# A two-layer decoder step on eight cores: all 2176 tokens resident, one pass over the weights, a column-tiled convolution and norm sums on VectorE

## The chip, the cores and the metric

The kernel runs on all eight cores of one Trainium2 chip: two dies, cores 0 to 3 and 4 to 7. Every core does the same work on its own tokens (one prompt of 2048 tokens and 16 samples of 8 tokens, so 2176), without exchange between cores. The metric is the time in microseconds (us) of the slowest core.

The chip has a second, slower state, in which the cores of one die show a lower granted TensorE clock, whatever the kernel: in e13's rounds the kernel before took 3559.17 us in one run, with clocks of 0.80 to 0.81 on one die and 0.96 on the other, and 3045.06 us in another; e1 took 3120.24 us with 0.84 and 0.98, and 2725.1 us with 0.98 on both.

Engines: PE is TensorE, PEld its weight loads, DVE VectorE, ACT ScalarE, POOL GpSimd, SP SyncE. In a line, the output stands left of the arrow.

## The reference, cut to what matters

```python
def trunk(x, p, ...):                     # 2 layers; D = 1024
    for i in range(2):
        x = x + 0.5 * swiglu(rmsnorm(x, norm_ffn[i, 0]), ...)      # width 2816
        h = rmsnorm(x, norm_mix[i])
        x = x + (even_mixer(h, ...) if i == 0 else odd_mixer(h, ...))
        x = x + 0.5 * swiglu(rmsnorm(x, norm_ffn[i, 1]), ...)
        gate = sigmoid(rmsnorm(x, norm_ple[i]) @ w_ple_gate[i])
        emb = rmsnorm(p[i] @ w_ple_proj[i], norm_ple_proj[i])
        x = x + gate * emb
    return rmsnorm(x, norm_final), ...    # and the new states

def even_mixer(h, ...):
    proj = h @ w_in                       # xa (512), va (512), ga (512)
    pa = <trailing means over 2, 4, 8, 16 tokens of xa, a 128x128 map per group, a scale>
    u = va * sigmoid(ga)
    conv = <causal depthwise convolution of u, 31 taps per channel>
    yb = silu(layernorm(conv + dw_bias))
    return concatenate([pa, yb]) @ w_out
```

Tokens lie along the free axis and channels on the partitions, so a sum over channels (every norm) runs over eight chunks and across partitions. The kernel before does all of it by eight ones-matmuls on TensorE; the changed one adds the chunks on VectorE and leaves one.

## The kernel before

It works in two token groups (1152 and 1024 tokens), each in three blocks, and streams all weights once for each group. The parts that the argument touches:

```python
# norm: eight squares on ScalarE, eight ones-matmuls, square root, reciprocal, eight scalings
def norm_squares(blk):
    for c in range(8):
        act(H[:, c, c0:c0 + n], X[:, c, c0:c0 + n], AF.Square)
def s_stats():
    mm_group(pb[:, 0:n], [(ONES[:, :], H[:, c, c0:c0 + n]) for c in range(8)])
    act(sd[:, 0:n], pb[:, 0:n], AF.Sqrt, bias=NORM_EPS, scale=1.0 / D)
    dve_recip(rs[:, 0:n], sd[:, 0:n])
# ... cut ...
# even mixer, convolution: 31 diagonal 128x128 matrices for each of four channel groups
for bi, (c0, n) in enumerate(blocks):
    for j in range(4):
        pairs = [(DIAG[:, j * 31 + k, :], UXP[:, j, c0 + k:c0 + k + n]) for k in range(31)]
        mm_group(pb[:, 0:n], pairs)
        # ... cut: V, VB (bf16 copy) and VSQ by three ScalarE instructions ...
    # ... cut: pooled projection, sums for the layer norm, layer norm ...
# ... cut ...
for g in range(2):                        # two token groups
    W.reset()                             # every weight is streamed again
    if g == 0:
        for blk in blocks:
            x_block_final(blk, "norm_ffn00")   # squares of all three blocks first
    for l in range(2):
        ffn(l, 0, ...); even_mixer(g, ...) or odd_mixer(g, ...); ffn(l, 1, ...); ple(l, ...)
```

Of the kernel before, what the change touches and what calls it, by code (L numbers as in the profile page):

```python
# [11 lines left out]
D = 1024  # L12
DFF = 2816
NHC = DFF // 128
SEQ = 2048
NS = 16
TS = 8
PLE = 256
GCOLS = [1024 + NS * TS, 1024]
GOFF = [0, GCOLS[0]]  # L20
TCOLS = sum(GCOLS)
MAXC = max(GCOLS)
SLOT = 3072
NSLOT = 6
NORM_EPS = 1e-6
LN_EPS = 1e-5
HPARTS = [list(range(0, 11)), list(range(11, 22))]

PCOL = {}
_pc = 0  # L30

def _padd(name, n):
    global _pc
    PCOL[name] = _pc
    _pc += n

# [12 lines left out]
_padd("dw_w", 4 * 31)  # L49
_padd("sc_w", 8 * 3)  # L50
_padd("ident", 128)
NPAR = _pc

def weight_tile_list():
    tiles = []
    for l in range(2):
        def ffn(f):
            for hp, part in enumerate(HPARTS):
                for m in part:
                    tiles.append((("gu", l, f, m), 8 * 256))  # L60
                for i in range(0, len(part), 3):
                    ch = part[i:i + 3]
                    tiles.append((("dn", l, f, tuple(ch)), len(ch) * 1024))
        ffn(0)
        if l == 0:
            for j in range(4):
                tiles.append((("ine_vg", j), 8 * 256))
            for j in range(2):
                tiles.append((("ine_xa", j), 8 * 256))
            tiles.append((("pp",), 4 * 128))  # L70
            for ch in ((0, 1, 2), (3, 4, 5), (6, 7)):
                tiles.append((("oute", ch), 8 * 128 * len(ch)))
        else:
            for c in range(8):
                tiles.append((("ino", c), 8 * 384))
            for ch in ((0, 1, 2), (3, 4, 5), (6, 7)):
                tiles.append((("outo", ch), 8 * 128 * len(ch)))
        tiles.append((("plep", l), 2 * 1024))
        ffn(1)
        for ch in ((0, 1, 2), (3, 4, 5), (6, 7)):  # L80
            tiles.append((("pleg", l, ch), 8 * 128 * len(ch)))
    return tiles

def _kc(w):
    k, n = w.shape
    return w.reshape(k // 128, 128, n).transpose(1, 0, 2)

def pack_weights(inp):
# [4 lines left out]
    for key, n in tiles:  # L93
# [10 lines left out]
        elif kind == "ine_vg":  # L104
# [3 lines left out]
                                _kc(w[:, 1024 + j * 128:1024 + (j + 1) * 128])], axis=2)  # L108
        elif kind == "ine_xa":
            j = key[1]  # L110
            w = inp["w_in_even"][0]
            t = _kc(w[:, j * 256:(j + 1) * 256])
# [14 lines left out]
        elif kind == "plep":  # L127
            t = _kc(inp["w_ple_proj"][key[1]])
        elif kind == "pleg":
# [8 lines left out]
    return out  # L138

def pack_params(inp):  # L140
# [17 lines left out]
    dw = inp["dw_weight"][0]  # L158
    p[:, PCOL["dw_w"]:PCOL["dw_w"] + 124] = dw.T.reshape(4, 128, 31).transpose(1, 0, 2).reshape(128, 124)
    sc = inp["sc_weight"][0]  # L160
    p[:, PCOL["sc_w"]:PCOL["sc_w"] + 24] = sc.T.reshape(8, 128, 3).transpose(1, 0, 2).reshape(128, 24)
    p[:, PCOL["ident"]:PCOL["ident"] + 128] = np.eye(128, dtype=np.float32)
    return p

def _fm(a):
    t, f = a.shape
    return a.T.reshape(f // 128, 128, t).transpose(1, 0, 2)

def pack_core(inp, i):
    xp = inp["x_prompt"][i]  # L170
    xs = inp["x_sample"][i * NS:(i + 1) * NS]
    xs_tm = xs.transpose(1, 0, 2).reshape(NS * TS, D)
    xT = np.concatenate([_fm(xp[:1024]), _fm(xs_tm), _fm(xp[1024:])], axis=2)
    pts = []
    for l in range(2):
        pp = inp["p_prompt"][l, i]
        ps = inp["p_sample"][l, i * NS:(i + 1) * NS].transpose(1, 0, 2).reshape(NS * TS, PLE)
        pts.append(np.concatenate([_fm(pp[:1024]), _fm(ps), _fm(pp[1024:])], axis=2))
    pT = np.stack(pts, axis=1)

    def st(a):
# [5 lines left out]
        "pT": np.ascontiguousarray(pT.reshape(128, 4, TCOLS), dtype=np.float32),  # L187
# [4 lines left out]

ENGS = ("pe", "act", "dve", "pool", "sp")
EPOCH = 30000

class Sched:
    def __init__(self):
# [7 lines left out]
        self.label = ""  # L205
        self.pe_labels = []
# [3 lines left out]
    def reg(self, handle, arena, base):  # L210
        self.arena[handle.name] = (arena, base, mybir.dt.size(handle.dtype))

    def region(self, ap):
        name = ap.tensor.name
        if name not in self.arena:
            return None
        arena, base, es = self.arena[name]
        pat = list(ap.ap)
        pstride = pat[0][0]
        off = ap.offset % pstride if pstride > 0 else ap.offset  # L220
# [3 lines left out]
        return arena, base + off * es, base + (off + ext) * es  # L224
# [35 lines left out]
    def op(self, eng, fn, reads=(), writes=(), dma_sem=None, extra_deps=(), dma_total=None):  # L260
# [11 lines left out]
        for ap in reads:  # L272
            r = self.region(ap)
            if r is not None:
                self._access(r[0], r[1], r[2], ticket, False, deps)
        for ap in writes:
            r = self.region(ap)
            if r is not None:
# [30 lines left out]

def build_program():  # L310
# [4 lines left out]

    d_xT = nc.dram_tensor("xT", [128, 8, TCOLS], F32, kind="ExternalInput").ap()
    d_pT = nc.dram_tensor("pT", [128, 4, TCOLS], F32, kind="ExternalInput").ap()
# [4 lines left out]
    d_gpr = nc.dram_tensor("gpprow", [128, 2, D], F32, kind="ExternalInput").ap()  # L322
    d_w = nc.dram_tensor("wts", [128, WTOT], F32, kind="ExternalInput").ap()
    d_yT = nc.dram_tensor("yT", [128, 8, TCOLS], F32, kind="ExternalOutput").ap()
# [10 lines left out]
    def alloc(name, shape, dt, arena=None, at=None):  # L335
        nbytes = int(np.prod(shape[1:])) * mybir.dt.size(dt)
        if at is None:
            off = cur[0]
            cur[0] += (nbytes + 63) // 64 * 64
            assert cur[0] <= top, (name, cur[0], top)  # L340
        else:
            off = at
        h = nc.alloc_sbuf_tensor_at(name, list(shape), dt, offset=off)
        S.reg(h, arena or "sb", off)
        return h

    X = alloc("x", [128, 8, MAXC], F32)
    H = alloc("h", [128, 8, MAXC], BF16)
    HID_BYTES = 11 * MAXC * 2
    hid_off = cur[0]  # L350
    HID = alloc("hid", [128, 11, MAXC], BF16)
    UXP = alloc("uxp", [128, 4, 30 + 1024], BF16, at=hid_off)
    o1 = (hid_off + 4 * (30 + 1024) * 2 + 63) // 64 * 64
    UXS = alloc("uxs", [128, 4, 38 * NS], BF16, at=o1)
    o2 = (o1 + 4 * 38 * NS * 2 + 63) // 64 * 64
    V = alloc("v", [128, 4, 512], F32, at=o2)
    assert o2 + 4 * 512 * 4 <= hid_off + HID_BYTES
    YCAT = alloc("ycat", [128, 8, MAXC], BF16, at=hid_off)
    RING = alloc("ring", [128, NSLOT, SLOT], BF16)
    DIAG = alloc("diag", [128, 4 * 31, 128], BF16)  # L360
    PT = alloc("pt", [128, 4, MAXC], BF16)
# [3 lines left out]
    IDB = alloc("idb", [128, 128], BF16)  # L365
    RC = alloc("rc", [128, 16], F32)
    vb_off = cur[0]
    VB = alloc("vb", [128, 4, 512], BF16)
    VSQ = alloc("vsq", [128, 4, 512], BF16)
    ESQ2 = alloc("esq2", [128, 8, 512], BF16, at=vb_off)  # L370
    STP = alloc("stp", [128, 4, 15 * NS], F32)
    STSC = alloc("stsc", [128, 8, 2 * NS], F32)
    PTAIL = alloc("ptail", [128, 4, 16], F32)
    UTAIL = alloc("utail", [128, 4, 32], BF16)
    ZTAIL = alloc("ztail", [128, 8, 2], F32)
    O_PS = alloc("o_ps", [128, 4, TS * NS], F32)
    O_DS = alloc("o_ds", [128, 4, TS * NS], F32)
    O_DP = alloc("o_dp", [128, 4, 32], F32)
    O_SS = alloc("o_ss", [128, 8, 2 * NS], F32)
    NSCR = 10  # L380
    SCW = 528
    SCR = [alloc(f"scr{i}", [128, SCW], F32) for i in range(NSCR)]
    RSE = alloc("rse", [128, MAXC], F32)
    LRS = alloc("lrs", [128, 512], F32)
    LRS2 = alloc("lrs2", [128, 512], F32)
    NRS = [alloc("nrs0", [128, 512], F32)] * 2
    nrs_i = [0]
    scr_i = [0]

    def scratch():  # L390
        t = SCR[scr_i[0] % NSCR]
        scr_i[0] += 1
        return t

    PS = []
    for i in range(8):
        p = nc.alloc_psum_tensor(f"ps{i}", [128, 512], F32)
        S.arena[p.name] = ("ps", i * 2048, 4)
        PS.append(p)
    ps_i = [0]  # L400

    def bank():
        p = PS[ps_i[0] % 8]
        ps_i[0] += 1
        return p
# [4 lines left out]
    def act(out, in_, func, bias=None, scale=None, extra_reads=()):  # L410
        kw = {}
        rd = [in_] + list(extra_reads)
# [8 lines left out]
        S.op("act", lambda e: e.activation(out=out, in_=in_, func=func, **kw), reads=rd, writes=[out])  # L421
# [9 lines left out]
    def dve_ts(out, in0, s1, s2, op0, op1=None):  # L431
        rd = [in0] + [s for s in (s1, s2) if s is not None and not isinstance(s, float)]
        if op1 is None:
            S.op("dve", lambda e: e.tensor_scalar(out=out, in0=in0, scalar1=s1, scalar2=None, op0=op0),
                 reads=rd, writes=[out])
        else:
            S.op("dve", lambda e: e.tensor_scalar(out=out, in0=in0, scalar1=s1, scalar2=s2, op0=op0, op1=op1),
                 reads=rd, writes=[out])

    def pool_tt(out, in0, in1, op):  # L440
        S.op("pool", lambda e: e.tensor_tensor(out=out, in0=in0, in1=in1, op=op), reads=[in0, in1], writes=[out])  # L441
# [3 lines left out]

    def dve_recip(out, in_):
        S.op("dve", lambda e: e.reciprocal(out=out, in_=in_), reads=[in_], writes=[out])  # L447
# [6 lines left out]
    def mm_group(ps_ap, pairs, extra_reads=()):  # L454
        n = len(pairs)
# [646 lines left out]
```

## Time and profile before

| | before |
|---|---|
| time, median of 4 runs | 3042.43 us (3040.2 to 3043.48) |
| profiled span, slowest core | 3043.2 us |
| PE busy | 2786.7 us, 92%, 17664 matmuls |
| PE idle | 256 us |
| VectorE, ScalarE busy | 1254.2 and 802.8 us |
| bytes read from memory by a core | 371 MB |

How to read it: PE is the engine to watch, because it is busy for 92% of the span. The kernel can only become faster by less PE work or by less PE idleness. The prediction below shows the lines.

### The profile page before, as it was taken

The numbers are of one execution on the slowest core, as the hardware profiler recorded it, in microseconds if no ns is written. First come the engines' busy times: TensorE is split into PE (matmuls) and PEld (weight loads), VectorE is DVE, ScalarE is ACT, GpSimd is POOL, SyncE is SP. The second block draws the span as 40 slices with busy tenths as digits, with TensorE's granted clock in tenths as the row PEclk, the third lists the DMA queues.
The fourth block names the chain that finished last, engine by engine and source line by source line (L and its number), as shares of the span: only waits on it lengthen the run. The fifth ranks groups of instructions, "written<-read, shape, count | busy, mean of one in ns | idle before, by whom it ended". The sixth has DMA issues, their size and how long they took to land.

```text
span 3043.2 us, 42462 instructions; the slowest of 8 cores (3031.3 to 3043.2 us)
## 1 busy us (share of the span) xinstructions
PE 2786.7 (92%) x17664; PEld 1499.0 (49%) x17664; DVE 1254.2 (41%) x2381; ACT 802.8 (26%) x1599; POOL 263.7 (9%) x407
## 2 busy tenths in 40 slices
PE   2999998999889999999973999989997999999996
PEld 0555443554445545455431555545554555555553
DVE  2432555232632257523354224552326222862335
ACT  2102344221330122321242112352224202232224
POOL 0000000000220000000031000000002100000003
PEclk7999998999999999999996999999999999999998
DMA  6433411534142534153325542405341534424332
GB/s 142 80 56 59 66 26 28 87 49 77 25 75 47 100 51 76 30 87 56 69 63 128 87 73 49 66 15 94 56 77 25 105 66 73 91 42 87 63 63 73
DMA packets 62495, 204.32 MB, mean 67 GB/s; under 512 B 8288, under 2 KB 15072, under 8 KB 62304
## 3 DMA queue, kind: packets, MB, share of 16 engines
q0 software_dynamic: 44592, 179.16, 34.5%
q1 hardware_dynamic: 17712, 22.45, 2.6%
q8 instruction: 139, 2.28, 0.3%
q14 instruction: 52, 0.43, 0.1%
HBM read 371.06 MB, written 10.62 MB: 125 GB/s over the span
## 4 chain that ended last, share of the span: by engine, by line
PE 82%; DVE 9%; ACT 3%; DMA 3%; issue 1%; SPq 1%; POOL 0%; ACTq 0%; DVEq 0%; POOLq 0%
PE ps L460 82%; DVE h L428 4%; DVE nrs_83 L447 2%; ACT h L421 2%; DMA x<-xT 2%; DVE x L428 1%; SPq L470 1%; DMA ring<-wts 1%; DVE x L424 1%; DVE lrs_82 L447 0%; DVE v L424 0%; ACT L421 0%; DVE ring L424 0%; POOL x L441 0%; ACT v L421 0%
## 5 line engine op out<-in xcount | busy, mean ns | idle before, releaser
L460 PE MATMUL ps<-h,ring 128*128 128x512 bf16 (+2 forms) x11352 | 1797.9, 320 | 56.5 <-DVE h L428 33.8
L460 PEld LDWEIGHTS ps<-h,ring 128*128 128x128 bf16 x11352 | 965.1, 99 | 871.7 <-issue 65.8
L460 PE MATMUL ps<-hid,ring 128*128 128x512 bf16 (+2 forms) x4224 | 656.7, 317 | 0.8 <-DVE hid L424 0.5
L460 PEld LDWEIGHTS ps<-hid,ring 128*128 128x128 bf16 x4224 | 356.1, 98 | 299.8 <-issue 1.1
L470 POOL DMA_DIRECT2D ring<-wts x298 | 157.8, 534 | 2539.3 <-PE ps L460 2504.3
L428 DVE SCALAR_TENSOR_TENSOR x<-ps,x 128x512 f32<-128x512 f32 (+2 forms) x384 | 200.0, 532 | 342.0 <-PE ps L460 339.2
L421 ACT ACTIVATE h<-x 128x512 bf16<-128x512 f32 (+2 forms) x432 | 200.4, 499 | 456.5 <-DVE x L428 269.0
L460 PE MATMUL ps<-h,ones 128*128 128x512 bf16 (+2 forms) x432 | 99.8, 389 | 142.4 <-ACT h L421 141.8
L428 DVE SCALAR_TENSOR_TENSOR h<-x,par,nrs_83 128x512 bf16<-128x512 f32 (+2 forms) x384 | 214.1, 606 | 1.7
L460 PEld LDWEIGHTS ps<-h,ones 128*128 128x128 bf16 x432 | 42.1, 115 | 192.5 <-ACT h L421 153.2
L421 ACT ACT_TABLE_LOAD x87 | 111.6, 1283 | 46.6 <-PE ps L460 44.3
L460 PE MATMUL ps<-pt,ring 128*128 128x512 bf16 (+2 forms) x384 | 80.9, 329 | 45.6 <-DVE ring L424 29.6
L460 PE MATMUL ps<-uxp,diag 128*128 128x512 bf16 (+2 forms) x620 | 108.5, 336 | 0.0
L421 ACT ACTIVATE scr_78<-ps 128x512 f32<-128x512 f32 (+2 forms) x91 | 42.1, 463 | 219.7 <-PE ps L460 211.4
L421 ACT ACTIVATE scr_76<-ps 128x512 f32<-128x512 f32 (+2 forms) x76 | 36.2, 476 | 233.9 <-PE ps L460 228.1
L421 ACT ACTIVATE scr_74<-ps 128x512 f32<-128x512 f32 (+2 forms) x87 | 41.3, 474 | 173.0 <-PE ps L460 164.8
L421 ACT ACTIVATE scr_72<-ps 128x512 f32<-128x512 f32 (+2 forms) x87 | 40.8, 469 | 169.5 <-PE ps L460 166.8
L421 ACT ACTIVATE scr_77<-ps 128x512 f32<-128x512 f32 (+2 forms) x90 | 42.5, 472 | 157.5 <-PE ps L460 148.8
L421 ACT ACTIVATE scr_79<-ps 128x512 f32<-128x512 f32 (+2 forms) x84 | 41.0, 488 | 156.7 <-PE ps L460 155.3
L421 ACT ACTIVATE scr_73<-ps 128x512 f32<-128x512 f32 (+2 forms) x90 | 41.9, 466 | 147.8 <-PE ps L460 139.3
L460 PEld LDWEIGHTS ps<-uxp,diag 128*128 128x128 bf16 x620 | 55.1, 97 | 52.3
L421 ACT ACTIVATE scr_70<-ps 128x512 f32<-128x512 f32 (+2 forms) x91 | 43.1, 474 | 136.6 <-PE ps L460 132.4
(261 smaller groups left out, 1361.1 us busy)
## 6 DMA issues: line engine op xcount, KB each, us to landing
ring<-wts POOLq DMA_DIRECT2D x216, 512.0 KB, 8.1
ring<-wts POOLq DMA_DIRECT2D x80, 768.0 KB, 7.2
x<-xT SPq DMA_DIRECT2D x32, 256.0 KB, 7.0
yT<-x SPq DMA_DIRECT2D x24, 256.0 KB, 2.1
yT<-x SPq DMA_DIRECT2D x8, 192.0 KB, 1.9
pt<-pT POOLq DMA_DIRECT2D x4, 288.0 KB, 22.6
pt<-pT POOLq DMA_DIRECT2D x4, 256.0 KB, 12.3
yT<-x SPq DMA_DIRECT2D x16, 64.0 KB, 1.6
```

Source lines behind the costliest of these rows:

```text
L421: S.op("act", lambda e: e.activation(out=out, in_=in_, func=func, **kw), reads=rd, writes=[out])
L424: S.op("dve", lambda e: e.tensor_tensor(out=out, in0=in0, in1=in1, op=op), reads=[in0, in1], writes=[out])
L428: S.op("dve", lambda e: e.scalar_tensor_tensor(out=out, in0=in0, scalar=scalar, in1=in1, op0=op0, op1=op1), reads=rd, writes=[out])
L447: S.op("dve", lambda e: e.reciprocal(out=out, in_=in_), reads=[in_], writes=[out])
L460: ins = e.matmul(ps_ap, l, r, start=(i == 0), stop=(i == n - 1))
L470: S.op(eng, lambda e: e.dma_start(out=out, in_=in_), reads=[in_], writes=[out], dma_sem=sem, dma_total=total, extra_deps=extra)
```

## The change

Its intent: to take matmuls away (convolution, norm sums, embedding norms), and to let tokens wait for nothing, by keeping all of them in SBUF in five blocks (four of 512 tokens, one of 128) and streaming each weight once. The program is emitted by a small scheduler: pieces of a norm are put on a heap with a model time and placed in the engines' queues when the modelled PE time has come (`defer`), or when the block is needed (`ensure`).

```diff
-        for c in range(8):                                   # norm before
-            act(H[:, c, c0:c0 + n], X[:, c, c0:c0 + n], AF.Square)
-            mm_group(pb[:, 0:n], [(ONES[:, :], H[:, c, c0:c0 + n]) for c in range(8)])
-            act(sd, pb, AF.Sqrt, ...); dve_recip(rs, sd)
+    class Norm:                                              # norm after
+        def chunk(self, mo, lag=0.8): ...                    # square, then:
+            dve_tt(self.acc[:, 0:n], self.acc[:, 0:n], sq[:, 0:n], ALU.add)
+            # ... after the eighth chunk one ones-matmul, then
+            act(rs[:, 0:n], self.pb[:, 0:n], AF.Abs_reciprocal_sqrt, bias=NORM_EPS)
 ...
+        def load_r(j, b):                     # even mixer: the shifted copy
+            for s in range(4):                # partitions 32s.. hold the row shifted by s
+                for q in range(4):            # 32 channels each
+                    items.append(("sp", RALL[32 * s:32 * s + 32, j, q, 0:L], src))
 ...
-                    pairs = [(DIAG[:, j * 31 + k, :], UXP[:, j, c0 + k:c0 + k + n]) for k in range(31)]
+                for m in range(8):            # 4 taps at once on the 4 x 32 input rows
+                    for q in range(4):        # 4 column tiles of 32 channels
+                        ops.append((pb[32 * q:32 * q + 32, 0:n], DG[:, 4 * j + q, m, :],
+                                    RALL[:, j, q, 4 * m * st:4 * m * st + n], m == 0, m == 7))
 ...
+                dve_copy(vv[:, 0, 0:n], V[:, j, 0:n])        # bf16 copy, now on VectorE
+                if b + 1 < NB:
+                    load_r(j, b + 1)
 ...
-    for g in range(2):
-        W.reset()
+    n0 = [Norm(b, "norm_ffn00") for b in range(NB)]
+    for mo in range(8):
+        n0[0].chunk(mo)
+    for b in range(1, NB):
+        for mo in range(8):
+            defer(6.0 + 12.0 * (b - 1) + 0.9 * mo, lambda b=b, mo=mo: n0[b].chunk(mo), ("n", b))
```

(The whole change touches most of the program.) The shifted copy is what the tiled convolution needs: a tile has 128 input rows for 32 channels, so each channel lies there four times, shifted by 0 to 3 tokens. A block takes 4 groups x 4 shifts x 4 parts = 64 small transfers inside SBUF, all issued through the SP queue.

## The prediction

> **What bounds the kernel now.** I read, in this order: the spans of all cores (3031.3 to 3043.2 us, dies alike, so no slow die), the page's busy times and 40 slices, the windows table in 50 us steps, the groups split by shape, the chain that ended last, and the timelines of the start, of the convolution and of the end.
>
> ```profile
> PE 2786.7 (92%) x17664; PEld 1499.0 (49%) x17664; DVE 1254.2 (41%) x2381; ACT 802.8 (26%) x1599; POOL 263.7 (9%) x407
> PE   2999998999889999999973999989997999999996
> ```
>
> TensorE (PE) is busy 92% of the span and idle 256 us. The row of slices shows where: the first slice, a hole near slice 21 (between the two token groups), and the last. The rest is lost at stage boundaries.
>
> ```profile
> 50.00:100.00 50.00, 34.49 (x202) 17.23 (x203) 29.67 (x72) 12.68 (x26) 1.50 (x3) 0.82 0.06 17
> ...
> 250.00:300.00 50.00, 50.00 (x293) 25.10 (x291) 11.90 (x21) 10.03 (x20) 2.11 (x4) 1.00 0.33 58
> ...
> 1600.00:1650.00 50.00, 7.93 (x59) 5.05 (x56) 19.03 (x23) 13.66 (x31) 9.06 (x15) 0.57 0.73 156
> ...
> 3000.00:3050.00 50.00, 24.62 (x174) 14.82 (x174) 27.05 (x43) 19.01 (x40) 13.86 (x16) 0.79 0.24 84
> ```
>
> Columns: stretch, then busy us (and instructions) of PE, weight load, VectorE (DVE), ScalarE (ACT), GpSimd; the clock; DMA share; GB/s. Inside a stage PE is full at clock 1.00 while DMA is a third used: matmul streaming is the bound, not weights. From these rows and their neighbours PE idles 59 us in 0 to 100, 49 us in 1600 to 1700 and 19 us after 3000; the other 130 us lie at about ten boundaries.
>
> ```profile
> 412.91 26.70 PEld L460 LDWEIGHTS ps<-uxp,diag 128*128 128x128 bf16 x124
> 413.12 26.98 PE L460 MATMUL ps<-uxp,diag 128*128 128x512 bf16 x124
> ...
> 443.20 7.09 PE L460 MATMUL ps<-uxs,diag 128*128 128x128 bf16 x124
> ```
>
> Start, duration, group. Here are my rates: 26.98 us / 124 = 217.6 ns for a matmul of 512 columns, 7.09 / 124 = 57.2 ns for 128 columns, in a straight line between them 164.1 ns for 384. Streamed columns set the time and narrow blocks cost nothing extra.
>
> ```profile
> 52.06 1.70 ACT L421 ACTIVATE h<-x 128x128 bf16<-128x128 f32 x8 [19.27 <-DMA x<-xT]
> ...
> 54.27 3.35 DVE L447 RECIPROCAL nrs_83<-scr_70 128x512 f32<-128x512 f32 x1 [39.97 <-ACT scr_70 L421]
> ```
>
> The start: block 0's inputs were in and squared by 17.6 us, but ScalarE, in order, stood waiting for the inputs of block 2 before it could take block 0's square root; the reciprocal waited 40 us for it. PE first runs full at 72 us. The chain has the same pattern at every boundary: squares, ones-matmul, root, reciprocal (3.35 us), scaling, and only then PE.
>
> [...]in seven long dense windows all eight cores have clock 1.00. So I let a fuller PE keep its clock. [...]no run here shows tiling yet. [...]the trace has 691 for its two-tensor multiplies. [...]issue time on the one queue is what I count for the new small transfers.
>
> **The change part by part.** Matmuls per token block. Before: four FFNs 4 x 528 = 2112; even mixer 64 + 32 + 4 + 124 convolution + 8 + 64 = 296; odd 256; embedding gates 160; embedding norms 48; nine norms of 8 = 72. Sum 2944, times 6 blocks = 17664, which the page confirms.
> 1. Convolution by column tiles: 31 diagonal 128x128 matmuls become 8 rounds of four 32-column tiles over a 4-fold shifted copy. With full concurrency 124 become 32.
> 2. Norm sums on VectorE: seven of nine norms need 1 ones-matmul for 8; two (after the gates) keep 8. 72 become 23.
> 3. Embedding norms by a Gram matrix: 48 become 12, plus 32 matmuls of 256 columns once (3.5 us).
> New sum: 2112 + 204 + 256 + 160 + 12 + 23 = 2767. Blocks: three of 512, one of 384, two of 128 become four of 512 and one of 128, the same 2176 columns.
> Before: 2944 x (3 x 217.6 + 164.1 + 2 x 57.2) ns = 2742 us. After: 2767 x (4 x 217.6 + 57.2) ns + 3.5 = 2570 us. **Matmul work falls by 172 us**: the convolution 92/177, the norms 49/177, the embeddings 36/177 of it. As PE is full inside stages, all of it is on the path.
> 4. One pass over weights, tokens resident: weight traffic halves, but DMA was not the bound, so that itself is worth little. What it removes is the 49 us hole at 1600 and half of the boundaries. With five blocks a block's norm has the time of the other blocks' down-projections and of the next stage's first tiles (3 x 16 x 217.6 ns = 10.4 us a block) to finish: tens of microseconds against a chain of 10 to 15. Those waits should vanish.
> 5. Start: squares go chunk by chunk, later blocks' norms come later. Block 0 was in at 13.4 us; then norm (5 us) and the first weight tile. Full-queue DMA moves 200 GB/s there (first window: 97% share), so I expect PE from about 21 us, starved of weight tiles to about 42, with 14 us done by then: 30 us lost (59 before).
> 6. End: last block's gate, norm, scaling, output: 15 us lost.
> 7. VectorE load: one add of 0.69 us for each 512-wide chunk. The reciprocals (3.35 us each, about 60) vanish into a ScalarE function. Per chunk in the last down-projection: residual 0.69 + add 0.69 + scaling 0.77 = 2.15 us against 11 x 0.2176 = 2.39 us of PE: fits. In the output projections PE has 8 x 0.2176 = 1.74 us: **VectorE becomes the bound there**. Odd: about 15.9 against 13.9 us a block, some 8 us in four blocks. Even, with layer norm: about 24.5 against 24 us; pooling about 8 against 7. I allow 20 us for these and 15 us for waits on weights, PSUM and shifted copies.
> 8. [...]
> 9. Cold clock after the start and the few gaps: PE busy before less the 2742 is 45 us; I keep 7.
> Sum: 2570 + 30 + 15 + 35 + 8 + 7 = 2665; I say **2660 us**, a fall of 12.6%.
>
> **The rivals.** (a) Column tiles do not overlap: 4 x 28 = 111 us of convolution, 83 us worse, about 2740. For it: each small matmul still has its own weight load, and 16 x 32 x 4 of them must be issued. [...] (b) Shifted copies bind: 64 transfers per block through one queue. Eight issues take 3.69 us:
>
> ```profile
> 1.06 3.69 SPq L470 DMA_DIRECT2D x<-xT  x8
> ```
>
> So 64 take 30 us at 0.46 us, against some 24 us of PE per block. The wait is per head group of 16, so the pipeline just holds; at 0.7 us an issue it costs about 20 us in each of three blocks, 60 us: 2720. (c) VectorE bursts: its average stays near 45%, but an in-order queue with norm work between PSUM drains may stop PE in every projection; two more microseconds in each of 45 block-stages is 90 us: 2750. (d) Denser PE lowers the clock: all stretches at 0.9 would give 2950. The dense windows speak against it. (e) Boundary waits vanish but weight waits at the ring replace them: ring 18 units, largest need 17; a few times 7 us, already allowed.
>
> **Range and chances.** The floor is 2570 plus some 35 us of start and end: 2605. Rivals (b) or (c) in part give 2700 to 2735; (a) whole gives 2740. Range **2605 to 2735**. Staying within 2% needs over 2980, more than (a), (b) and (c) together (2660 + 80 + 60 + 90 = 2890), so only (d) could: faster 0.98, same 0.015, slower 0.005.
>
> **What would show it.** Right: PE instructions about 14350; PE busy near 2600, 97 to 98% of the span; no hole at mid-span; clock 1.00 in dense windows; the convolution 30 to 40 us in all. VectorE busy about 1200 us, reciprocals gone, highest in the output projections. DMA bytes about half. Wrong: slices below 9 in the even mixer with PE waiting for DMA into the shifted copy (b); PE waiting for VectorE on PSUM (c); rounds of four far above 218 ns (a); clock below 1.00 inside stages (d).

Step 8: 8 us for column tiles that do not quite overlap; the kernel before has no such tiles, so its traces could not show it. The sum has this term: 2570 + 30 + 15 + 35 + 8 + 7 = 2665, and without it 2657, beside the 2660 that I said. That denser work lowers the clock, rival (d), was an assumption that no trace of the kernel before shows. The "691" is ns, for one instruction of 512 columns. "Nothing extra" for narrow blocks holds to 5%: 4 x 57.2 = 228.8 ns against 217.6. The cold clock of step 9 is in the traces of the kernel before: 0.57 from 1600 to 1650 us, and after a gap that ended at 1595.6 us weight loads 0.43 us apart, where the dense ones above are 0.22 apart.

## The result, and the profile after

The changed kernel takes **2760.45 us** (median of 4 runs, 2759.11 to 2761.99), the kernel before 3042.43. The ratio is 0.9075 (95% interval 0.9062 to 0.9088). The direction was right, the size was not: 282 us gained, not 382, and 2760 lies above the range of 2605 to 2735.

The page of the changed kernel: busy times, the slices of PE and of its clock, and the chain that ended last.

```profile
span 2759.2 us, 35204 instructions; the slowest of 8 cores (2746.5 to 2759.2 us)
...
PE 2592.8 (94%) x14347; PEld 1250.6 (45%) x14347; DVE 1151.8 (42%) x2089; ACT 701.3 (25%) x1248; POOL 87.4 (3%) x167
...
PE   4699999978759999999999999999999999999997
...
PEclk9899999998879999999999999999999999999999
...
PE 84%; DVE 6%; SPq 4%; ACT 2%; issue 2%; DMA 1%; POOL 0%; DVEq 0%; ACTq 0%; POOLq 0%
```

PE did what was foretold: 14347 matmuls, 2592.8 us busy. The hole at mid-span is gone. But PE is idle for 166 us, and the row of slices shows where: the first two slices, and slices 9 to 12, which are the even mixer. The queue of SP has a share of 4% in the chain, which it had no reason to have. The windows table puts numbers to it (stretch, then busy us and instructions of PE, weight load, DVE, ACT, POOL; clock; DMA share; GB/s):

```profile
0.00:150.00 150.00, 91.90 (x442) 42.44 (x443) 60.54 (x121) 46.18 (x80) 7.24 (x17) 0.86 0.55 116
...
550.00:850.00 300.00, 218.83 (x1556) 99.85 (x1554) 152.90 (x325) 112.17 (x192) 7.63 (x14) 0.84 0.33 68
850.00:1350.00 500.00, 500.00 (x2742) 245.36 (x2740) 168.36 (x295) 95.43 (x174) 20.90 (x39) 1.00 0.21 36
...
2650.00:2760.00 110.00, 90.93 (x536) 45.67 (x533) 89.61 (x166) 62.26 (x111) 1.09 (x2) 0.94 0.29 94
```

Idle at the start 58 us, in the even mixer 81 us, in the last stretch 19 us; 9 us everywhere else together. The second and third of these rows are the picture of the kernel: 73% full at clock 0.84 for the 300 us of the even mixer, then full for 500 us at 1.00.

The start, in PE's timeline (start, duration, group, and in brackets the idle time before it and what ended that):

```profile
23.43 15.35 PE L538 MATMUL ps<-h_48,ring 128*128 128x512 bf16 x64 [8.01 <-DVE h_48 L511]
...
52.33 16.26 PE L538 MATMUL ps<-h_49,ring 128*128 128x512 bf16 x64 [9.12 <-DVE h_49 L511]
...
82.31 0.61 PE L538 MATMUL ps<-sq_88,ones 128*128 128x512 bf16 x1 [11.00 <-DVE sq_88 L507]
89.03 11.28 PE L538 MATMUL ps<-h_50,ring 128*128 128x512 bf16 x39 [6.11 <-DVE h_50 L511]
```

PE starts at 23 us, as foretold (21). But each block's 64 products are followed by a gap, 13.5 us before block 1 and 20 us before block 2, and what ends them is a norm (scaled `h`, or the sum `sq`). The inputs were there: the weight queue, which is made to wait for them, went on at 23.7 (block 1), 42.4 (block 2) and 51.4 us (block 3).

The even mixer, in the table of what PE waited for between 550 and 850 us (total, times, longest), and then the SP queue's timeline:

```profile
PE ps L538 <- DMA rr<-u: 20.8, 4, 7.5
PE ps L538 <- DMA rr<-us: 17.6, 2, 9.0
PE ps L538 <- DVE sq_86 L507: 14.1, 1, 14.1
PE ps L538 <- DVE pt_74 L525: 9.5, 2, 5.5
```

```profile
692.60 85.14 SPq L562 DMA_DIRECT2D rr<-u  x128
777.85 43.55 SPq L562 DMA_DIRECT2D rr<-us  x64
```

For 129 us SP does nothing but issue shifted copies, back to back (the table of its queue's waits is empty for this stretch): 85.14 / 128 = **0.665 us each**, so 42.6 us a block, beside some 24 us of PE work. That is rival (b) of the prediction, with almost the pessimistic figure (0.7). The next line of the waits is one that I had not seen coming; the timelines of DVE and of PE show it:

```profile
579.71 0.66 DVE L516 TENSOR_SCALAR us<-us 128x1920 bf16<-128x1920 bf16 x1 [22.61 <-DMA us<-st_dw]
```

```profile
582.82 0.26 PE L538 MATMUL ps<-sq_86,ones 128*128 128x128 bf16 x1 [14.13 <-DVE sq_86 L507]
```

VectorE stood 22.6 us at the head of its queue before a doubling of the samples' convolution state, whose load was still under way. The norm sums of the sample block stood behind it, and PE behind those.

The convolution itself, however, is as good as it could be (PE's timeline):

```profile
636.46 5.36 PE L538 MATMUL ps<-rr,ring 128*32 128x512 bf16 x96
```

96 tiles are 24 rounds of four; 5.36 / 24 = 223 ns, against 217.6 for one full matmul. Four column tiles run nearly in the time of one (2% more).

### The profile page after: what moved, and what is told of

Read it like the earlier page. It is cut to its first block, busy times and chain, and to the rows that moved or that the text cites. A ratio compares the mean times of both kernels' runs of the same rounds, so it can differ in the third digit from the quotient of the medians.

```text
span 2759.2 us, 35204 instructions; the slowest of 8 cores (2746.5 to 2759.2 us)
## 1 busy us (share of the span) xinstructions
PE 2592.8 (94%) x14347; PEld 1250.6 (45%) x14347; DVE 1151.8 (42%) x2089; ACT 701.3 (25%) x1248; POOL 87.4 (3%) x167
## 4 chain that ended last, share of the span: by engine, by line
PE 84%; DVE 6%; SPq 4%; ACT 2%; issue 2%; DMA 1%; POOL 0%; DVEq 0%; ACTq 0%; POOLq 0%
PE ps L538 84%; SPq L562 4%; DMA us<-st_dw 1%; DVE h_50 L511 1%; ACT L499 1%; DVE h_49 L511 1%; DVE h_48 L511 1%; DVE scr_91 L507 0%; DVE h_51 L511 0%; DMA xscr_70<-st_sc 0%; DVE scr_93 L507 0%; DVE x_43 L511 0%; DVE scr_95 L507 0%; DVE x_46 L511 0%; DVE scr_92 L511 0%
## 5 line engine op out<-in xcount | busy, mean ns | idle before, releaser
L538 PE MATMUL ps<-h_49,ring 128*128 128x512 bf16 x1892 | 430.5, 381 | 11.6 <-DVE h_49 L511 9.1
L538 PE MATMUL ps<-h_48,ring 128*128 128x512 bf16 x1892 | 430.0, 381 | 10.5 <-DVE h_48 L511 8.0
L538 PE MATMUL ps<-h_50,ring 128*128 128x512 bf16 x1892 | 430.6, 382 | 8.5 <-DVE h_50 L511 6.1
L538 PE MATMUL ps<-h_51,ring 128*128 128x512 bf16 x1892 | 428.5, 381 | 1.6 <-ACT h_51 L501 1.6
L538 PEld LDWEIGHTS ps<-h_49,ring 128*128 128x128 bf16 x1892 | 185.8, 98 | 237.6 <-DVE h_49 L511 9.4
L538 PEld LDWEIGHTS ps<-h_50,ring 128*128 128x128 bf16 x1892 | 186.1, 98 | 236.1 <-DVE h_50 L511 6.6
L538 PEld LDWEIGHTS ps<-h_51,ring 128*128 128x128 bf16 x1892 | 185.5, 98 | 226.0 <-ACT h_51 L501 2.5
L538 PEld LDWEIGHTS ps<-h_48,ring 128*128 128x128 bf16 x1892 | 181.9, 98 | 215.5 <-issue 13.3
L501 ACT ACTIVATE scr_95<-ps 128x512 f32<-128x512 f32 (+1 forms) x130 | 74.2, 571 | 418.6 <-PE ps L538 395.2
L538 PE MATMUL ps<-hid_54,ring 128*128 128x512 bf16 x736 | 163.7, 379 | 0.0
L538 PE MATMUL ps<-hid_56,ring 128*128 128x512 bf16 x736 | 163.7, 379 | 0.0
L538 PE MATMUL ps<-hid_55,ring 128*128 128x512 bf16 x736 | 163.7, 379 | 0.0
L538 PE MATMUL ps<-hid_53,ring 128*128 128x512 bf16 x736 | 162.8, 379 | 0.0
L562 POOL DMA_DIRECT2D ring<-wts x152 | 80.9, 538 | 2423.9 <-PE ps L538 2327.9
L501 ACT ACTIVATE scr_92<-ps 128x512 f32<-128x512 f32 (+1 forms) x136 | 72.6, 534 | 326.7 <-PE ps L538 320.0
L501 ACT ACTIVATE scr_91<-ps 128x512 f32<-128x512 f32 (+1 forms) x133 | 74.7, 562 | 288.9 <-PE ps L538 282.3
L501 ACT ACTIVATE scr_94<-ps 128x512 f32<-128x512 f32 (+1 forms) x125 | 65.2, 521 | 311.5 <-PE ps L538 306.4
L538 PE MATMUL ps<-h_52,ring 128*128 128x128 bf16 x1892 | 128.3, 224 | 12.0 <-DVE scr_91 L511 4.0
L538 PEld LDWEIGHTS ps<-h_52,ring 128*128 128x128 bf16 x1892 | 118.1, 100 | 35.2 <-DVE scr_91 L511 4.3
L501 ACT ACTIVATE scr_93<-ps 128x512 f32<-128x512 f32 (+1 forms) x130 | 61.1, 470 | 217.7 <-PE ps L538 214.6
L507 DVE TENSOR_TENSOR hid_55<-ps,scr_91 128x512 bf16<-128x512 f32 x61 | 42.2, 692 | 167.9 <-PE ps L538 167.9
L538 PEld LDWEIGHTS ps<-hid_55,ring 128*128 128x128 bf16 x736 | 72.0, 98 | 86.6
```

The source lines that it names most:

```text
L501: return e.activation(out=out, in_=in_, func=func, **kw)
L507: S.op("dve", lambda e: e.tensor_tensor(out=out, in0=in0, in1=in1, op=op), reads=[in0, in1], writes=[out])
L538: ins = e.matmul(o_, l, r, start=st, stop=sp)
L562: S.op(eng, lambda e: e.dma_start(out=out, in_=in_), reads=[in_], writes=[out], dma_sem=sem, dma_total=total, extra_deps=extra)
```

## The experiments

All are edits of the changed kernel. "The changed kernel's dies" below are its two die medians in four runs, 2753.5 to 2757.5 us.

The changed kernel was not run again beside its edits, and they ran on other chips, so a difference of a few us needs a control. I cut each trace at two matmuls: the last that reads `hid` (the hidden values of an FFN, the `swiglu` of the reference) before the first that reads the shifted copy `rr` (the end of the first FFN), and the first that reads `hid` after the last that reads `rr`. So the middle part is the even mixer and the second FFN's products before its first `hid`, which are alike in all runs. Medians of the undisturbed dies, in us:

| | up to the mixer | mixer part | the rest |
|---|---|---|---|
| changed kernel | 555 to 556 | 455 to 458 | 1743 to 1745 |
| e1 | 553 | 421 to 423 | 1743 |
| e2 | 551 to 552 | 439 to 440 | 1744 |
| e3 | 550 | 456 to 459 | 1744 |
| e4 | 553 | 456 to 458 | 1744 |
| e10 | 515 | 394 | 1744 |
| e12 | 521 | 386 | 1763 |
| e13 (same kernel as e10) | 511 to 512 | 389 | 1745 |

The rest is the same on all chips where no edit touches it, so the chips may be compared. The other two parts are less steady: the first is 551 to 553 us in e1, e2 and e4, which change nothing in it, and one kernel (e10, e13) differs by 3 and 5 us on two chips. A gain of 5 us or less between chips is therefore unclear.

### e1: one copy for four channel groups

```diff
-            for s in range(4): for q in range(4): RALL[32s.., j, q, 0:L]            # at each j
+            if j % 4 != 3: return
+            for s in range(4): for q in range(4): RALL[32s.., j0:j0 + 4, q, 0:L]    # 16 a block
```

> Edit: each shifted copy for the convolution now carries all four channel groups in one transfer, so 16 transfers a block in place of 64, the same bytes; they are issued when the block's last convolution is through. Result stays right. Theory A (issue time): in the changed kernel the queue issued one copy each 0.665 us (85.14 us for 128), 42.6 us a block, against some 24 us of TensorE work; with 16 issues it is about 11 us, which fits under the 14.7 us of pooling and output projection between two convolutions. The 38.4 us that TensorE waited for the copies vanish, and with the warmer clock the time falls by 45 to 60 us, to about 2705. Rival B (bytes or rows): an issue costs by its rows, four times as many here, so a block still takes 42 us, now all exposed after the last convolution: 2760 to 2800.

Measured: correct. One of six runs was fast, 2725.1 us; in the other five one die was held back, and the other die's median was 2718.2 to 2724.2 in all of them. So the gain is some 36 us by the undisturbed dies and 35 by the one fast run. The SP queue and the window of the mixer:

```profile
617.46 11.03 SPq L562 DMA_DIRECT2D rr<-u  x16
```

```profile
550.00:850.00 300.00, 243.21 (x1679) 115.02 (x1702) 168.64 (x360) 123.98 (x212) 9.17 (x17) 0.89 0.39 74
```

A transfer of four times the bytes is issued in 11.03 / 16 = 0.69 us, nearly the 0.665 of a small one. PE's waits for the copies are gone. What follows: here the number of transfers cost the time, not their bytes. The gain was below the 45 to 60 that I expected, because other waits took part of it: the bf16 copy on VectorE (20.8 us in five waits, where the changed kernel has 9.5 in two) and, still, the samples' state (13.6 us).

### e2: the doubling of the samples' state later

```diff
-        dve_ts(US[:, :, 0:30 * NS], US[:, :, 0:30 * NS], 2.0, ALU.mult)      # at the mixer's head
         # ... value and gate products of all blocks ...
+        dve_ts(US[:, :, 0:30 * NS], US[:, :, 0:30 * NS], 2.0, ALU.mult)
```

> Edit: the doubling of the sample convolution state on VectorE is moved from the start of the even mixer to the end of its first projection. Theory: at 558 to 580 us VectorE stood 22.6 us in front of this one instruction, waiting for a transfer that can only be issued once the hidden buffer is free, and TensorE[...] stood 14.1 us and then ran 3.4 us at half clock. The time falls by 14 to 18 us, to about 2744. Rival: the copies behind it set the pace of the stage anyway, so the gain is lost there: within 3 us of 2760.

Measured: 2739.5 us (2738.59 to 2741.41), ratio to before 0.8988 (0.8974 to 0.9001) against 0.9075: 21 us less. By the table 16 to 18 of them are in the mixer; the others lie before it, where the edit changes nothing. The wait of 14 us is gone, and the clock in the mixer's window rose from 0.84 to 0.88. So the theory holds, with its 14 to 18 us; the few us beyond the wait's length go with the warmer clock (in the changed kernel 0.54 for the 3.5 us after this wait, then 1.00), which I did not test by itself.

### e3: other times for the first norms

```diff
-            defer(6.0 + 12.0 * (b - 1) + 0.9 * mo, ...)
+            t0, dt = ((0.0, 0.25), (9.0, 1.3), (21.0, 1.0), (33.0, 0.9))[b - 1]
+            defer(t0 + dt * mo, ...)
```

> Edit: the first norms of blocks 1 to 4 are put into the queues earlier (start 0, 9, 21, 33 us after the first tile in place of 6, 18, 30, 42). Theory: TensorE stood 13.5 us at 39 to 52 us and 20 us at 69 to 89 us because the squares and sums of the next block were queued behind the activations of the tiles before, though the inputs of blocks 1 to 3 had landed by 24, 42 and 51 us. The time falls by 20 to 38 us, to about 2730. Rival: the inputs' transfers set the start (the 16 DMA engines are 97% busy in the first 50 us), and nothing moves: within 5 us of 2760.

Measured: fast runs 2752.03 to 2757.17 us, ratio 0.9032 (0.9014 to 0.905). That is some 6 us less, hardly more than the spread between chips, so the theory's 20 to 38 us did not come. PE's timeline shows why:

```profile
24.59 0.61 PE L538 MATMUL ps<-sq,ones 128*128 128x512 bf16 x1 [9.19 <-DVE sq L507]
35.77 28.97 PE L538 MATMUL ps<-h,ring 128*128 128x512 bf16 x118 [10.57 <-DVE h L511]
...
83.47 26.86 PE L538 MATMUL ps<-h,ring 128*128 128x512 bf16 x108 [8.50 <-DVE h L511]
```

The gap before block 1 went, but only because block 0 now starts at 35.8 us: block 1's pieces had been placed in the queues before block 0's scalings. The edit moved the gap. It was a bad experiment for its question.

### e4: the pooled projection ahead of the convolution

```diff
         for b in range(NB):
+            pp(b)
             if b + 1 < NB:
                 conv(b + 1)
-            pp(b)
```

> Edit: the pooling projection of a block is issued ahead of the next block's convolution in place of right before the output projection that reads it. Under theory A (issue time of the copies sets the pace of the stage) the 2 us that TensorE waits for ScalarE in each of five blocks is not on the path: TensorE waits longer for the copies, and only the last block or two gain, 2 to 6 us in all: about 2756. Rival C: these waits count as they stand, 11 us: about 2749.

Measured: 2757.71 us (2757.07 to 2759.52), ratio 0.9047 (0.9034 to 0.9061): 3 us less, and by the table none of it in the mixer, so no gain is shown. PE's waits for `h` fell from 11.4 to 3.6 us, but others came in their place (for ScalarE's `scr` 13.7 us after 7.8, for VectorE's `x` 7.4 after none), and those for the copies stayed (37 us after 38). Both new waits are still there in the repaired kernel (14.6 and 7.2 us in e13); whether this edit helps it is not shown.

### e5: every copy cut in two

```diff
-                    items.append(("sp", RALL[32 * s:32 * s + 32, j, q, 0:L], src))
+                    h = L // 2
+                    items.append(("sp", RALL[32 * s:32 * s + 32, j, q, 0:h], src[:, 0:h]))
+                    items.append(("sp", RALL[32 * s:32 * s + 32, j, q, h:L], src[:, h:L]))
```

> The changed kernel with each of a block's 64 shifted copies cut into two halves of the row: the same bytes, twice the instructions on the sync engine's queue. Theory A (in the even mixer the issuing of the copies sets the pace, a fixed 0.66 us each): a block goes from 43 to some 85 us of issuing, so the four blocks after the first cost about 4 x 42 = 170 us more, 2900 to 2940 us. Rival (the landing of the bytes, or the memory's bandwidth, is what the convolution waits for): the same bytes, within 20 us of 2760. Rival (issue time goes with the bytes): about 2760 as well, with issues of 0.33 us, which the profile would show.

Measured: correct; fast runs 2945.61, 2947.4 and 2948.6, ratio 0.9672 (0.9652 to 0.9693): some 187 us more. The SP queue:

```profile
761.25 165.39 SPq L562 DMA_DIRECT2D rr<-u  x256
926.80 82.03 SPq L562 DMA_DIRECT2D rr<-us  x128
```

165.39 / 256 = 0.646 us for half the bytes, again without a wait on the queue. With e1, a factor of eight in bytes per transfer (16.9 KB to 135 KB) leaves the issue time at 0.65 to 0.69 us. Theory A holds (6 to 9 us above its range), both rivals fall: the stage's time follows the count of transfers issued on the one queue.

### e6: the convolution as 31 whole matmuls, copies as they are

```diff
-                for m in range(8): for q in range(4): ops.append((pb[32q..], DG[...], RALL[...], ...))
+                for m in range(31):
+                    ops.append((pbo, W.get(("diag",))[:, 128 * m:128 * m + 128], RALL[...], m == 0, m == 30))
```

The weights are stale, the result wrong.

> The changed kernel with each convolution group as 31 whole 128x128 products in place of 32 column tiles in eight rounds; the weights are stale on purpose, so the result is wrong. Matmul work grows by 4 x 23 x 216 ns = 19.9 us in each of the four large blocks and 5 in the last: 85 us. Theory A (the copies of the next block take 43 us to issue beside some 24 us of TensorE work, which becomes 44): nearly all of it fits under the copies, +5 to +25 us, 2765 to 2785. Rival (the tiled convolution is worth its matmul time even here): +85, about 2845.

Measured: fast runs 2786.61 and 2786.07, ratio 0.9142 (0.9122 to 0.9162): 26 us more (expected 5 to 25) for 85 us more of matmuls (the expectation's estimate). PE now waits for no copy at all in the mixer; instead SP's queue waits 10.5 us for PE, to have read a copy before it is overwritten. So in the changed kernel, tiling the convolution was worth 26 of its 85 us: the copies that it needs gave the rest back.

### e7: the first norm finished before the others are planned

```diff
+    ensure(("n", 0))
     for b in range(1, NB):
         for mo in range(8):
-            defer(6.0 + 12.0 * (b - 1) + 0.9 * mo, ...)
+            t0, dt = ((0.0, 0.3), (17.0, 0.4), (27.0, 0.6), (36.0, 0.6))[b - 1]
+            defer(t0 + dt * mo, ...)
```

> The changed kernel with the first norm's pieces finished before those of blocks 1 to 4 are planned, and these planned from the moment TensorE starts (0, 17, 27 and 36 us, when their inputs have landed) instead of 6, 18, 30 and 42. Theory A (the gaps of 13.5 and 20 us before blocks 1 and 2 are norm chains that begin too late): both gaps fall below 5 us, 25 to 33 us gained, 2728 to 2737. Rival (the inputs set the start: block 2 lands at 42 us, block 3 at 51): the first gap closes but the second stays, at most 15 us gained, 2745 to 2752.

Measured: one fast run, 2755.91 us, and a **wrong** result (relative error 0.028). From the code, and not tested: when the buffers of the squares run out, the scheduler places a later piece inside an earlier one, and a block's sum can then be closed before all its squares are in it. The time is of use all the same:

```profile
74.29 0.61 PE L538 MATMUL ps<-sq,ones 128*128 128x512 bf16 x1 [7.95 <-DVE sq L507]
84.53 25.67 PE L538 MATMUL ps<-h,ring 128*128 128x512 bf16 x108 [9.63 <-DVE h L511]
```

Block 3's sum stands in PE's queue before block 2's products; its squares stand behind block 2's on ScalarE. Block 2 waits for block 3's norm. This is neither the inputs nor a late plan: it is the order in the queues. By the letter of my expectation the rival came nearer, by its reason it did not.

### e8: all repairs, with the start of e7

```diff
+            act(vv[:, 0, 0:n], pb[:, 0:n], AF.Identity, bias=pcol("dw_bias", j), scale=0.5)
-            dve_copy(vv[:, 0, 0:n], V[:, j, 0:n])
```

added to the edits of e1, e2, e4 and e7.

> All repairs in one: one copy carries four channel groups, the doubling of the sample state after the value and gate products, the pooled projection ahead of the convolution, the new start, and the bf16 copy for the layer norm's sums on ScalarE instead of VectorE. If the gains add: 35 + 20 + 3 + 30 + 10 = about 98 us, 2660. If they overlap (the sample state's wait, once gone, uncovers another wait of VectorE in the mixer): 2680 to 2700.

Measured: fast runs 2689.78, 2688.03 and 2709.59 (three of four), ratio 0.8845 (0.8804 to 0.8886), with the wrong result of e7's start. The gains of the mixer's repairs add up to about this (71 us); the start gives nothing, as in e7.

### e9: the first norm's pieces in a fixed order

```diff
-            defer(...)                        # the heap of the changed kernel
+    ensure(("n", 0))
+    n0[1].sums()                              # squares and adds of block 1, before any product
     # in the loop over product groups t of block bb:
+                    if bb + 1 < NB and t == 1:
+                        first[bb + 1].scaled()   # ones-matmul, root, eight scalings
+                    if bb + 2 < NB and t == 3:
+                        first[bb + 2].sums()
```

> The changed kernel with the first norm's pieces put into the engines' queues in a fixed order: the squares and sums of block b+2 behind block b's fourth product group, the sum's matmul and the scalings of block b+1 behind block b's second. Theory A (at the start it is the order of the pieces in the in-order queues that leaves the gaps, of 13.5 and 20 us, and not the arrival of the inputs, which are there at 24, 42 and 51 us): both gaps fall below 5 us together, 25 to 33 us gained, 2728 to 2737 and correct. Rival (the inputs, or the VectorE work of a block's norm, some 11 us, set the pace): at most 12 us gained, 2748 or more.

Measured: correct. The chip's second die was held back in every run, of the kernel before too, so there is no ratio. In four of five runs the first die was undisturbed, with medians of 2714.3 to 2716.2, against 2753.5 to 2757.5: **40 us less**. PE's timeline, on a core with a lowered clock:

```profile
22.90 10.83 PE L538 MATMUL ps<-h,ring 128*128 128x512 bf16 x32 [7.27 <-DMA ring<-wts]
...
33.83 16.98 PE L538 MATMUL ps<-h,ring 128*128 128x512 bf16 x64
...
50.89 16.98 PE L538 MATMUL ps<-h,ring 128*128 128x512 bf16 x64
```

No gap is left between the blocks, with inputs arriving as before. Theory A holds; that it gave 40 and not 33 fits the clock, which no longer falls at the start (below, in e13's window, 1.00 against 0.86).

### e10 and e13: all repairs, with this start

The edits of e1, e2, e4, e8's line and e9.

> All repairs with this start in place of the earlier one: merged copies, sample state doubled later, pooled projection earlier, bf16 copy on ScalarE, ordered first norm. The set with the faulty start took 2689. If the gain of the start (25 to 30) adds: 2660 to 2665. If the ordered start only moves the gaps: 2685 to 2690.

> The repaired kernel again, hoping for an undisturbed chip. Its undisturbed die showed a median span of 2652 us, where the changed kernel has 2755. Theory A (the causes found are the whole shortfall against 2660): 2652 to 2662 in fast runs, ratio to before 0.871 to 0.874. Rival (the undisturbed die gained from the other die's being held back): 2670 or more.

Measured: e10 fell on the chip with the held-back die; all six runs were slow, and in five of them the first die's median was 2650.2 to 2652.1. e13 on another chip: **2649.07 us** (2648.25 to 2649.95, five fast runs), ratio to before 0.8694 (0.8679 to 0.8709), correct. It is 3 us under theory A's range, and beats both kernels: 13% below the kernel before, and by the two ratios 4.2% below the changed one. The rival, that a held-back die helps the other, falls. Its page and two windows:

```profile
PE 2570.3 (97%) x14347; PEld 1246.4 (47%) x14347; DVE 1146.9 (43%) x2069; ACT 713.2 (27%) x1270; POOL 87.6 (3%) x167
...
PE   6999999997899999999999999999999999999997
```

```profile
0.00:150.00 150.00, 127.75 (x672) 61.10 (x673) 70.11 (x135) 56.62 (x97) 8.28 (x19) 1.00 0.60 124
550.00:850.00 300.00, 274.50 (x1926) 133.04 (x1924) 157.90 (x317) 134.91 (x235) 8.91 (x16) 0.95 0.39 73
```

Idle at the start fell from 58 to 22 us, in the mixer's window from 81 to 26, and PE's busy time by 22 us for the same number of matmuls, as the granted clock was higher in both windows (1.00 for 0.86 and 0.95 for 0.84).

### e11: the 31 whole matmuls on the repaired kernel

e6's edit on e10's kernel. Its output is wrong, which doesn't matter for the time.

> The same repaired kernel with each convolution group as 31 whole products (stale weights, a wrong result on purpose). On the changed kernel as it was, this cost 26 us of the 85 that the matmuls count. Theory A (the copies hid it there, and no longer do): +70 to +85 us over the repaired kernel. Rival (something else of the mixer, ScalarE or VectorE, sets its pace even with the copies merged): +25 to +50.

Measured: all six runs slow; the undisturbed first die 2717.3 to 2719.2, against 2650.2 to 2652.1 of e10 on the same chip: 67 us more, 3 short of theory A and well above the rival. The tiling that was worth 26 us is worth 67 once its copies no longer bind. The 18 us short of 85 go with waits that the longer convolution hides (idle in the mixer's window 18 us, for 29) and a warmer clock there (0.97 for 0.94; PE is busy 73 us longer, not 85); I did not separate the two.

### e12: the norm sums back on TensorE, on the repaired kernel

```diff
+            if gname != "norm_ffn00":
+                mode = "pe"                   # eight ones-matmuls instead of adds on VectorE
```

> The repaired kernel with six of the seven norms that sum on VectorE back to eight ones-matmuls a block: 42 more a block set, 42 x (4 x 216 + 57 ns) = 39 us of TensorE. Theory A (what leaves TensorE leaves the time, step 2 of the prediction): +35 to +40 us. Rival (VectorE's adds cost waits at the block boundaries that eat part of the gain): +15 to +25.

Measured: correct; all six runs slow; the undisturbed first die 2669.2 to 2672.6: **20 us more**, half of the 39. Theory A falls and the rival stands, with its figure. On one core of that die PE is busy 30 us longer (2604.5 for 2574.1) but idle 13 us less (66.7 for 79.5), 7 of it in the mixer's window:

```profile
550.00:850.00 300.00, 271.03 (x1886) 130.71 (x1885) 156.44 (x316) 133.99 (x233) 8.50 (x16) 0.94 0.38 73
```

```profile
550.00:850.00 300.00, 278.17 (x1968) 131.61 (x1967) 139.94 (x283) 134.87 (x236) 8.50 (x16) 0.97 0.40 73
```

The first row is e10, the second e12. With the adds on VectorE, PE waits there 7.0 us for VectorE's residual add (`DVE x`), which e12 does not show. The table of stages says where the other half of the 39 us went: of e12's 42 matmuls a block set, 7 fall before the mixer, 7 in it and 28 after, 6, 6 and 26 us by count; measured are 7 more, 8 *less* and 19 more. So (by one profile of each) the adds on VectorE are a loss in the mixer and a gain elsewhere. That busy time grew by 30 and not 39 goes with the clock of that window (0.97 for 0.94; 3% of 300 us would be 9 us, an estimate); I did not test that part by itself.

### e14: the bf16 copy back on VectorE

> The repaired kernel with the bf16 copy for the layer norm's sums back on VectorE. Theory A (behind the pooling work in VectorE's queue it holds back the sums' matmul that stands between two convolution groups): +8 to +15 us over e13. Rival (ScalarE is as late, the wait only changes its name): within 4 us of e13.

Measured: all four runs counted as fast, but three had cores with a lowered clock (0.979 to 0.983): 2658.29 to 2683.1 us, ratio 0.8769 (0.8717 to 0.8821). Where a die was undisturbed its median was 2652.1 to 2655, against 2644.1 to 2645.6 of e13: 8 us, the lower edge of theory A. The wait that comes back in PE's table:

```profile
PE ps L538 <- DVE pt L525: 8.2, 2, 6.4
```

## Why the prediction was right or wrong

**Where the missing 95 us are.** The prediction's sum was 2665, with the 8 us of step 8. PE's busy time came 8 us above its terms (2592.8 against 2570 + 8 + 7); as the 8 us of step 8 were not needed, I put what is left, some 23 us and not 7, down to step 9, the cold clock. The trace shows it after PE's gaps: 0.50 from 52.3 to 55.8 us, 0.83 in the next 3.5 us and 1.00 from 59.3 to 68 us (block 1), 0.50, 0.71 and 1.00 in the same way from 89 us (block 2). The start lost 58 us, not 30. The end lost 18 to 19, not 15. Steps 4 and 7 allowed 35 us for all else, and it was 90, of which 81 in the even mixer. 8 + 28 + 3 + 55 = 94, and 2665 + 94 = 2759.

**Steps 1 to 3, the matmuls: right.** The count of 14350 was 14347, and PE's busy time fell by 194 us. The convolution's tiles overlap nearly fully (223 ns a round, 217.6 for one full matmul), so rival (a) fell, and **step 8**, 8 us for tiles that do not quite overlap, was not needed. They kept PE busy for 43.9 us in the changed kernel, where the clock in the mixer is 0.84 (30 to 40 expected). (The rival's "16 x 32 x 4" small matmuls count the four tiles twice; there are 640.) But the sentence "as PE is full inside stages, all of it is on the path" failed for the new kernel: e6 shows that only 26 us of the convolution's gain reached the time, e11 that 67 do once the stage is PE-bound, and e12 that on the repaired kernel the norm sums are worth 20 of 39.

**Step 4, boundaries: right outside the start and the even mixer.** The mid-span hole is gone, and all the rest of the span has 9 us of PE idleness.

**Step 5, the start: the step failed, by 28 us.** PE did begin at 23 us. I then wrote that it would be starved of weight tiles; it was not. It waited for the norms of blocks 1 and 2. I had counted when the inputs arrive and what a norm costs, but not in which order the pieces stand in in-order queues. e9 changes only that order and wins 40 us; e3 and e7 show that moving the planned times does little (5 to 6 us) as long as one block's sum can stand in front of another block's products. The kernel before has the same fault in another form (its root waiting behind block 2's squares), and I had read it there.

**Step 7, the even mixer: the term was mis-sized, and this is rival (b).** The mechanism was named, with the right question (0.46 or 0.7 us an issue). I took 0.46, from transfers of 256 KB over 128 partitions, for transfers of 34 KB over 32. (The view that it came from had a warning that I passed over: the next 16 of the same transfers took 12.87 us, 0.80 each.) Measured: 0.665, so 43 us a block against 24 of PE. e1 (a quarter of the issues) wins 36 us, e5 (twice the issues, the same bytes) loses 187. Even at 0.7 I put the cost at 60 us more than 2660, and the measured loss through the copies was smaller than that, because other waits took part of it (e1). The 20 us that this step gave to VectorE in the output projections were hardly used: in the odd mixer's stretch, 1900 to 2150 us, PE idled under 3 us.

**What no step had:** the samples' state at the head of VectorE's queue, 16 to 18 us in the mixer (e2); the bf16 copy moved to VectorE, 8 us (e14). These are rival (c) in kind, an in-order queue that stops PE, but not in place: I looked for it in the projections, where nothing happened.

**Do the causes suffice?** One by one, 40 + 36 + 17 + 8 = 101 us; together, 2760 - 2649 = 111 us between different chips (44 before the mixer, 67 in it). The 10 us between the two sums I can't place: e4's edit may give something once the copies no longer bind, and the spread between chips is up to 5 us a part. The repaired kernel stands at 2649, 11 us below the predicted 2660. So what the prediction priced was there to be had; what it missed was order in queues and the number of transfers. The rival (d), a lower clock, did not occur in fast runs: from 900 to 1300 us all eight cores of the changed kernel had 1.00, with PE 99 to 100% busy. So dense work alone did not bring it; what starts the slower state no run here shows. Left open: the repaired kernel is still idle for 22 us at the start, 26 in the mixer and 18 at the end, and I did not try to take these away; nor did I test what made e7's result wrong, or whether issuing the small copies from a second engine's queue does as well as merging them.

## What to carry to other kernels

Count the transfers of a stage and multiply by the issue time of transfers of the same shape; if that exceeds the stage's matmul time, as 64 x 0.665 = 42.6 us did some 24 us here, look at the count first: merging the transfers won 36 us, and halving them with twice the count lost 187. In a program whose engines take their work in order, ask of every instruction that can wait for a transfer or for another block what stands behind it: here VectorE stood 22.6 us before one doubling and PE 14.1 us behind it, and the order of the first norms' pieces was worth 40 us. Matmuls removed from a stage may not count fully where something else in that stage takes nearly as long: of an estimated 85 us of convolution, 26 counted beside the copies, and 67 without their bound.
